# Where warming transposes, a masked copy, a run of products and a price in the planner stand: a two-layer hybrid encoder on one core

## The chip, the core and the metric

The kernel runs on one core of a Trainium2 chip. Five engines run side by side, each with its own queue in which instructions start in order: TensorE (PE: matrix products and transposes, with PEld for the loading of the stationary operand), VectorE (DVE), ScalarE (ACT), GpSimd (POOL) and SyncE (SP), which here issues the DMAs. TensorE writes to PSUM; VectorE and ScalarE read it there. Semaphores order the engines among each other. The metric is the device time of one execution in microseconds (us), lower is better.

## The reference

The trunk takes `x` of 512 frames by 1024 and puts 16 meta tokens in front of them (the zero pads of the reference need no work). It runs two layers, each a normed input projection, two groups of mixers, SiLU gates, an output projection and a residual, and ends with a norm.

```python
for layer in range(DEPTH):                     # DEPTH = 2
    hn = rms_norm(h, norm_g[layer])
    if layer % 2 == 0:
        out = layer_ab(hn, ...)                # top-k sparse attention (A) and gated linear attention (B)
    else:
        out = layer_cd(hn, ...)                # retention (C) and stick-breaking attention (D)
    h = h + jnp.where(valid[None, :, None], out, 0.0)
return rms_norm(h[:, PAD_FRONT + N_META:], final_g)
```

The change touches the chunked recurrences of B and C. B, cut to its core (C is alike, with a fixed decay and a layer norm of each head):

```python
def gla_chunked(q, k, v, log_a):               # 4 heads, chunks of 64, dk = 64, dv = 128
    bcum = jnp.cumsum(log_a, axis=3)
    q_t, k_t = q * jnp.exp(bcum), k * jnp.exp(-bcum)
    att = jnp.where(causal, jnp.einsum('bhncd,bhnsd->bhncs', q_t, k_t), 0.0)
    o_intra = jnp.einsum('bhncs,bhnse->bhnce', att, v)
    contrib = jnp.einsum('bhncd,bhnce->bhnde', k * jnp.exp(b_last - bcum), v)
    _, S_before = lax.scan(lambda S, inp: (S * inp[0][..., None] + inp[1], S), S0, (decay, contrib))
    o_inter = jnp.einsum('bhncd,bhnde->bhnce', q_t, S_before)
    return o_intra + o_inter
```

## The kernel before

**Layout.** All activations lie transposed: features on the 128 partitions, T = 528 tokens (16 meta, 4 blocks of 128 frames) along the free dimension, in two halves of 272 and 256. Each fp32 operand of a projection is split into a high and a low fp32r part, and a product is three: high by high, low by high, high by low (`begin` and `project`, from L603). The weights come as raw tiles by DMA; ScalarE makes the high part `wh`, VectorE the low part `wl` (`split_next`, L577).

**Recording and planning.** The program isn't issued as it is written. `Recorder.add` (L174) records each operation with what it reads and writes, and `price` (L216) gives it a cost in ns; for TensorE `o.mm` holds the rows, whether it is plain fp32, and the time after which the next one can start. A PSUM tile counts as one region in the dependencies, so whatever reads or writes any part of it stands in order with a write by another engine. `order` (L286) then plays all five engines forward in a list schedule: of the instructions that are ready on an engine it takes the one that can start first (on TensorE with a `MARGIN` of 300 ns, and 2000 ns of preference for the same rows, `STAY`), and among those the one that is due earliest. `LAT` is added between engines. An instruction on VectorE, ScalarE or GpSimd may start before the one ahead of it has ended, by `OVER` (84, 103 and 60 ns). A kind of tile has a fixed number of buffers, which go round in recorded order. What comes out is the order of the instructions on each engine; their waits are then made from the real dependencies. So a price changes no instruction, but it can change the order of all of them.

**Tiles of PSUM.** `acc` has 2 buffers of 1024 columns; `s()` and `tr()` share kind `x` with 3 buffers, and `pv()` is kind `y` with one buffer (L498).

**The start.** `consts` (L673) records 46 (`WARM`, L496) transposes of the identity into a y tile that nobody reads; they keep TensorE busy while the input comes. `load_x` (L728) then loads the meta tokens and `x` by rows, squares and norms them, turns the rows of the norm weights (`rows`, a tile from two DMAs of `norm_g` and `gla_gate_b`) with one transpose into `gains` (L789 to 791), and turns the 16 groups of `x` (`turn`), where ScalarE and VectorE apply the gains and make `hh` and `hl`.

**Layer one** runs the index scores, then top-k on VectorE (`topk`, rounds of MAX8 and MATCH_REPLACE8 on the tiles `score`, which the profile calls lt), while TensorE goes on with the values, the four heads of gated linear attention and their projections. Then come the eight heads of attention in pairs. In `gla_steps` (L1355) each head makes `att` (masked with `copy_predicated`), turns its keys, does the meta tokens in one tile `m` (a product, a masked copy into `attm`, a transpose of the meta keys into another part of `m`, a copy of it into `ktm`, then two products with the meta values `vm`), makes the states `ss` in seven dependent steps on VectorE (the profile calls them st, read from `x`), and sums the two parts of the output in a y tile:

```python
m = self.tr()
nc.tensor.matmul(m[:NMETA, 0:16], ks[:, :NMETA], qs[:, :NMETA], start=True, stop=True)
nc.vector.copy_predicated(attm[:NMETA], self.tri[:NMETA, :NMETA], m[:NMETA, 0:16])
self.transpose(m[:NMETA, 384:512], kh[:, :NMETA])
```

**Layer two** has retention heads (`retention_steps`, L1582) between pairs of stick-breaking heads, with the same two products per block: `av` by `vt` (the profile: y<-gv,wt) and `qx` by `ss` (y<-st,st). An fp32 product is two records in the profile.

As the recorder issues everything from one place, all instructions have line L406 in the profile; they are told apart by their tiles.

Of the kernel before, what the change touches and what calls it, by code (L numbers as in the profile page):

```python
# [16 lines left out]
P = 128  # L17
DM = 1024
KT = DM // P
NMETA = 16  # L20
SEQ = 512
T = NMETA + SEQ
NB = SEQ // P
# [15 lines left out]
def blk(b):  # L39
    return slice(NMETA + P * b, NMETA + P * (b + 1))  # L40
# [126 lines left out]
class Recorder:  # L167
# [48 lines left out]
    def price(self, o):  # L216
        o.mm, o.port = None, False
        n = max([x.free() for x in o.ins + o.outs] or [1])
        sbuf = not any(x.tile.psum for x in o.ins)
        scalar = 65 if any(isinstance(x, View) and x.free() == 1 for x in o.ins) and n > 1 else 0  # L220
        if o.eng == "tensor":
            lhs, rhs = (o.args[1], o.args[2]) if len(o.args) > 2 else (o.kw["lhsT"], o.kw["rhs"])
            turn = o.name == "transpose"
            plain = rhs.dtype == F32
            k, m, n = lhs.shape[0], lhs.free(), rhs.free()
            two = plain and not turn
            o.mm = (32 if k <= 32 else 64 if k <= 64 else P, plain, max(n * 0.45 * (2 if two else 1) + 4, 107 * m / P + 4) + (107 if two and n <= P else 0))
            o.cost = max(273, 170 + 0.4375 * n) if not two else 180 + 1.62 * n
        elif o.eng == "scalar":
            o.cost = (205 if sbuf else 165) + 0.83 * n + (80 if isinstance(o.kw.get("bias"), View) or isinstance(o.kw.get("scale"), View) else 0)  # L230
            if "accum_out" in o.kw:
                o.cost += 200
        elif o.eng == "vector":
            o.port = sbuf and o.name not in ("max", "match_replace")
            if o.name == "tensor_tensor_scan":
                o.cost = 144 + 2.1 * n
            elif o.name in ("tensor_scalar", "tensor_copy") and sbuf:
                o.cost = 160 + 0.52 * n + scalar
            elif o.name == "memset":
                o.cost = 100 + 0.3 * n  # L240
            else:
                o.cost = 148 + 1.05 * n + scalar
            if o.name == "tensor_tensor_reduce" or "accum_out" in o.kw:
                o.cost += 80
            if o.name == "match_replace":
                o.cost += 70
        elif o.eng == "gpsimd":
            o.cost = {"memset": 92 + 0.84 * n, "tensor_tensor": 178 + 2.17 * n}.get(o.name, 194 + 1.5 * n)
        else:
            x = o.outs[0] if o.outs else o.ins[0]  # L250
            kb = n * x.shape[0] / 256
            o.cost = kb * 3.6


    LAT = {"tensor": 55, "vector": 33, "scalar": 34, "gpsimd": 60, "sync": 27}
    OVER = {"vector": -84, "scalar": -103, "gpsimd": -60}
    SWITCH, ROWS = 80, 95
    MARGIN = 300
    STAY = 2000
# [26 lines left out]
    def order(self):  # L286
# [10 lines left out]
        wire = 0.0  # L297
        begun = {}
        result = []

        def ready(o):
            est = 0.0
# [13 lines left out]
        while left:  # L316
            best = None
            for e, xs in lists.items():
                pick = None
                base = free[e] + (last.mm[2] if e == "tensor" and last is not None else 0)  # L320
                for o in xs:
                    est = o.est
                    ok = True
                    for t in o.tiles:
                        if t.slot:
                            continue
                        k = t.kind
                        if t.at != k.next or not k.free:
                            ok = False
                            break  # L330
                        est = max(est, min(k.free)[0] + self.LAT[e])
                    if not ok:
                        continue
                    now = free[e] + (self.slot(last, o) if e == "tensor" and last is not None else 0)
                    start = max(est, now)
                    pri = o.pri
                    if e == "tensor" and last is not None:
                        pri -= self.STAY if o.mm[0] == last.mm[0] else 0
                    key = (max(est + (self.MARGIN if e == "tensor" else 0) - base, 0.0), pri)
                    if pick is None or key < pick[0]:  # L340
                        pick = (key, start, o)
                if pick and (best is None or pick[1] < best[1]):
                    best = pick
            assert best, "no instruction can be placed"
            _, start, o = best
            e = o.eng
            lists[e].remove(o)
            cost = o.cost
            if e == "vector" and o.port and begun.get("pool", (0, 0))[0] < start < begun.get("pool", (0, 0))[1] - 100:
                cost += begun["pool"][1] - start - 70  # L350
            if e == "gpsimd" and begun.get("port", (0, 0))[0] < start < begun.get("port", (0, 0))[1] - 100:
                cost += begun["port"][1] - start - 100
            end = start + cost
            if e == "vector" and o.port:
                begun["port"] = (start, end)
            ends[o] = end
            o.begin, o.end = start, end
            if e == "tensor":
                free[e], last = start, o
            elif e == "sync":  # L360
                free[e] = start + 430
                wire = end = max(wire, start + 1900) + o.cost
                if o.outs and o.outs[0].tile.whole and o.ins and o.ins[0].tile.whole:
                    end = start + 6900
                ends[o] = o.end = end
            else:
                free[e] = end + self.OVER[e]
                if e == "gpsimd":
                    begun["pool"] = (start, end)
            for t in o.tiles:  # L370
                k = t.kind
                if not t.slot:
                    t.slot = min(k.free)
                    k.free.remove(t.slot)
                    k.next += 1
            for t in o.tiles:
                t.left -= 1
                t.ends = max(t.ends, end)
                if not t.left:
                    t.kind.free.append((t.ends, t.slot[1]))  # L380
            result.append(o)
            left -= 1
            for q in o.succs:
                q.wait -= 1
                if not q.wait:
                    ready(q)
# [23 lines left out]
class Kernel:  # L410
# [82 lines left out]


    XL, XC, XN, XW, PW, PL = 2, 9, (0, 1, 1, 2), (1, 4, 7, 10, 13), 0, 0
    WARM = 46  # L496

    LAG = {"a": 5, "d": 6, "t": 1, "v": 4, "n": 9, "s": 6, "k": 11}  # L498
    TOPY = 3
# [173 lines left out]
    def consts(self):  # L673
        nc, ins = self.nc, self.ins
# [1 line left out]
        self.ident = self.cp.tile([P, P], F32, name="ident")  # L676
        make_identity(nc.core, self.ident.real)

        warm = self.pv()
        for _ in range(self.WARM):  # L680
            self.transpose(warm[:, :P], self.ident)
        self.one = self.cp.tile([P, 1], F32, name="one")
        nc.vector.memset(self.one, 1.0)
        self.eps = self.cp.tile([P, 1], F32, name="eps")
# [2 lines left out]
        self.gains = self.cp.tile([P, 18], F32, name="gains")  # L687
        self.g = self.gains[:, :16].rearrange("p (l k) -> p l k", l=2)
        self.gb = self.gains[:, 16:18]

    def late_consts(self):
        nc, ins = self.nc, self.ins
# [35 lines left out]
    def load_x(self):  # L728
        nc, ins = self.nc, self.ins
# [59 lines left out]
        t = self.tr()  # L789
        self.transpose(t[:, :18], rows)  # L790
        nc.scalar.copy(self.gains, t[:, :18])
        self.split_next()
        todo = [(g, t0, k, c) for g, t0, c in ((first, 0, self.HALVES[0]), (second, T0, self.HALVES[1]))
                for k in range(KT)]
# [560 lines left out]
    def gla_steps(self, head, r, v, gates, ep, qs, ks, kh):  # L1355
        nc = self.nc
# [17 lines left out]

        m = self.tr()
        nc.tensor.matmul(m[:NMETA, 0:16], ks[:, :NMETA], qs[:, :NMETA], start=True, stop=True)
        nc.vector.copy_predicated(attm[:NMETA], self.tri[:NMETA, :NMETA], m[:NMETA, 0:16])
        self.transpose(m[:NMETA, 384:512], kh[:, :NMETA])
        ktm = self.ktm[head % 2][:, :64]
        nc.vector.tensor_copy(ktm[:NMETA], m[:NMETA, 384:448])  # L1380
        yield self.LAG["t"]
# [21 lines left out]
        o = self.pv()  # L1403
        ov = o.rearrange("p (b e) -> p b e", b=NB)
        for b in range(NB):
            c = slice(P * b, P * (b + 1))
            nc.tensor.matmul(ov[:, b], att[:, b], vt[:, c], start=True, stop=False)
            nc.tensor.matmul(ov[:, b], qs[:, blk(b)], ss[:, c], start=False, stop=True)
        on = self.head_norm(ov, P, False)
        yield self.LAG["n"]  # L1410
        while not gates:
# [170 lines left out]
    def retention_steps(self, head, r, v, gates, q, k, qx, kz, kzm, turned):  # L1582
# [27 lines left out]
        o = self.pv()  # L1610
        ov = o.rearrange("p (b e) -> p b e", b=NB)
        for b in range(NB):
            c = slice(P * b, P * (b + 1))
            nc.tensor.matmul(ov[:, b], av[:, b], vt[:, c], start=True, stop=False)
            nc.tensor.matmul(ov[:, b], qx[:, c], ss[:, c], start=False, stop=True)
        on = self.head_norm(ov, P, True)
        yield self.LAG["n"]
        while not gates:
# [213 lines left out]
```

## Time and profile before

| what | us |
|---|---|
| median of 3 runs | 649.28 (648.82 to 650.77) |
| the profiled execution | 647.35 |
| its span, from first to last instruction | 645.6 |

The profile describes the execution of 647.35 us. Its last stretch and the largest wait by total:

```profile
580.00:645.60 65.60, 59.02 (x292) 48.55 (x290) 33.76 (x56) 28.51 (x63) 5.96 (x4) 0.97 0.33 113
```

```profile
POOL pm L406 <- ACT wt L406: 90.3, 18, 22.6
```

The first line is a stretch of the span in us: its length, then busy time and number of instructions of PE, PEld, DVE, ACT and POOL, the clock that TensorE was granted (1.00 is full), the share of the DMA engines and GB/s. The second says who waited for whom, with total, number and longest wait in us; idle time of an engine that isn't the bound, as POOL here, costs nothing. Matmuls are pipelined, and the end of one is modelled, so those that follow each other overlap in the records. A timeline row has the start, the duration, the engine, the operation, the tiles written and read, and in brackets how long the engine stood idle before it and what released it; "x3" means three such instructions in a row.

### The profile page before, as it was taken

What the parts mean: (1) busy time and instruction counts of PE and PEld (TensorE: products, weight loads), DVE (VectorE), ACT (ScalarE), POOL (GpSimd) and SP (SyncE); (2) the same over time, 40 slices, a digit from 0 to 9 for tenths busy, and PEclk for the clock granted to TensorE, in tenths of its full rate; (3) what the DMA queues carried; (4) which work ended last, traced back from release to release, by engine and by line L of the source; (5) the groups of instructions that cost most, each with busy time, mean ns of one, the idle gap of its engine ahead of it and who ended that gap; (6) DMA issues with size and microseconds to landing.
All of it is one profiled execution on the core that took longest, in us unless ns stands there. A gap on an engine that the chain in (4) does not pass through costs nothing. (4 is left out here: it accounts for less than half of the span.)

```text
span 645.6 us, 12173 instructions
## 1 busy us (share of the span) xinstructions
PE 620.5 (96%) x4393; PEld 569.2 (88%) x4393; DVE 491.6 (76%) x1142; ACT 412.9 (64%) x936; POOL 77.5 (12%) x185
## 2 busy tenths in 40 slices
PE   7999999899899999999899999989999999999995
PEld 6979999789889999999899999878888878988884
DVE  6768799999997786879732854789965689978443
ACT  5656562352344878799733775899854699956234
POOL 4001101100000111212121200000400010310030
PEclk9899999999999999999999999999999999999998
DMA  8437223222223323121243362103222203144503
GB/s 260 96 89 233 66 67 83 66 69 77 73 62 83 102 67 83 51 66 50 84 133 99 116 209 85 50 17 103 79 85 65 81 2 98 45 120 147 164 16 130
DMA packets 91103, 59.24 MB, mean 92 GB/s; under 512 B 7314, under 2 KB 81628, under 8 KB 91044
## 3 DMA queue, kind: packets, MB, share of 16 engines
q1 hardware_dynamic: 91044, 58.48, 31.6%
q8 instruction: 34, 0.56, 0.4%
q14 instruction: 25, 0.20, 0.1%
HBM read 53.18 MB, written 6.90 MB: 93 GB/s over the span
## 5 line engine op out<-in xcount | busy, mean ns | idle before, releaser
L406 PE MATMUL acc<-hh,wh 128*128 128x272 f32 (+2 forms) x968 | 243.7, 311 | 2.3 <-ACT hh L406 1.7
L406 PE MATMUL acc<-hl,wh 128*128 128x272 f32 (+2 forms) x968 | 236.1, 304 | 0.5 <-DVE hl L406 0.5
L406 PE MATMUL acc<-hh,wl 128*128 128x272 f32 (+2 forms) x968 | 232.6, 302 | 0.0
L406 PEld LDWEIGHTS acc<-hh,wh 128*128 128x128 f32 x968 | 159.1, 189 | 9.0 <-ACT hh L406 2.1
L406 PEld LDWEIGHTS acc<-hl,wh 128*128 128x128 f32 x968 | 158.1, 189 | 4.7 <-DVE hl L406 1.2
L406 PEld LDWEIGHTS acc<-hh,wl 128*128 128x128 f32 x968 | 157.1, 189 | 5.4
L406 ACT ACTIVATE wh<-raw 128x512 fp32r<-128x512 f32 x154 | 96.4, 630 | 101.8 <-PE acc L406 86.3
L406 DVE TENSOR_TENSOR wl<-raw,wh 128x512 fp32r<-128x512 f32 x154 | 106.1, 696 | 49.0 <-ACT wh L406 45.1
L406 ACT ACTIVATE wt<-x 128x272 f32<-128x272 f32 (+3 forms) x100 | 42.8, 451 | 29.5 <-PE x L406 15.9
L406 PE MATMUL x<-st,st 128*128 128x272 f32 (+6 forms) x240 | 51.3, 291 | 0.4 <-DVE ptm L406 0.2
L406 ACT ACTIVATE wt<-wt 128x528 f32<-128x528 f32 (+3 forms) x74 | 43.9, 603 | 8.7 <-DVE wt L406 7.7
L406 PE MATMUL x<-ident,wt 128*128 128x128 f32 (+1 forms) x296 | 45.3, 275 | 1.9 <-ACT wt L406 1.1
L406 PEld LDWEIGHTS x<-st,st 128*128 128x128 f32 (+2 forms) x240 | 37.4, 186 | 9.2 <-ACT wt L406 3.1
L406 PEld LDWEIGHTS x<-ident,wt 128*128 128x128 f32 (+1 forms) x296 | 33.8, 139 | 6.5 <-DVE ptm L406 1.9
L406 ACT ACTIVATE wt<-wt,tiny 128x272 f32<-128x272 f32 (+6 forms) x64 | 34.5, 561 | 7.8 <-POOL tiny L406 5.8
L406 ACT ACTIVATE st<-acc 64x528 fp32r<-64x528 f32 (+1 forms) x58 | 34.8, 599 | 1.3 <-DVE lt L406 0.4
L406 PE MATMUL y<-pt,vt 128*128 128x256 f32 x192 | 30.8, 283 | 1.9 <-ACT pt L406 1.8
L406 DVE TENSOR_TENSOR pt<-x,pt 128x384 fp32r<-128x384 f32 (+1 forms) x48 | 28.3, 595 | 4.7 <-ACT pt L406 4.3
L406 DVE TENSOR_TENSOR_SCAN wt<-wt,wt 128x64 f32<-128x64 f32 (+5 forms) x50 | 30.6, 657 | 0.1
L406 PEld LDWEIGHTS y<-pt,vt 128*128 128x128 f32 x192 | 26.0, 189 | 4.7 <-ACT pt L406 2.2
L406 POOL COPY pm<-wt 128x16 f32<-128x16 f32 x32 | 12.8, 419 | 140.1 <-ACT wt L406 90.3
L406 ACT ACTIVATE wt<-wt,one 128x528 f32<-128x528 f32 (+3 forms) x42 | 29.5, 703 | 0.2
(204 smaller groups left out, 922.1 us busy)
## 6 DMA issues: line engine op xcount, KB each, us to landing
raw<-in_w_in_ab_dram SPq DMA_DIRECT2D x64, 256.0 KB, 2.8
raw<-in_w_in_cd_dram SPq DMA_DIRECT2D x56, 256.0 KB, 2.9
raw<-in_w_out_ab_dram SPq DMA_DIRECT2D x16, 256.0 KB, 2.8
raw<-in_w_out_cd_dram SPq DMA_DIRECT2D x16, 256.0 KB, 2.7
rep<-rows SPq DMA_DIRECT2D x8, 328.0 KB, 5.9
lt<-rep SPq DMA_DIRECT2D x8, 264.0 KB, 2.7
pt<-in_x_dram SPq DMA_DIRECT2D x8, 256.0 KB, 4.4
wt<-in_x_dram SPq DMA_DIRECT2D x8, 256.0 KB, 3.1
```

The source lines that it names most:

```text
L406: getattr(getattr(self.core, o.eng), o.name)(*[bind(x) for x in o.args], **{k: bind(x) for k, x in o.kw.items()})
```

## The change

It has four parts.

1. `WARM` becomes two numbers, 26 and 20. A new function `warm(i)` records that many transposes of the identity into a y tile; `consts` calls it for the 26, and `load_x` for the 20, after the gains' transpose and its copy. In `price`, a transpose into a y tile takes 160 ns of TensorE instead of the 111 that the formula gives.
2. In `gla_steps`, the transpose of the meta keys is recorded before the masked copy of the same tile `m`.
3. In `gla_steps` and `retention_steps`, the four products with the values come first and the four with the states after them, instead of in turn. Only the first product of the bank has the start mark.
4. `order` remembers which PSUM tiles the last instruction on VectorE and on ScalarE read (`reads`). Where the next one reads the same tile, its start moves by 98 ns on VectorE and by 115 ns on ScalarE (`SAME`).

```diff
@@ -226,6 +226,8 @@
             two = plain and not turn
             o.mm = (32 if k <= 32 else 64 if k <= 64 else P, plain, max(n * 0.45 * (2 if two else 1) + 4, 107 * m / P + 4) + (107 if two and n <= P else 0))
             o.cost = max(273, 170 + 0.4375 * n) if not two else 180 + 1.62 * n
+            if turn and o.outs[0].tile.kind.tag == "y":
+                o.mm = (P, plain, 160)
         elif o.eng == "scalar":
             o.cost = (205 if sbuf else 165) + 0.83 * n + (80 if isinstance(o.kw.get("bias"), View) or isinstance(o.kw.get("scale"), View) else 0)
             if "accum_out" in o.kw:
@@ -254,6 +256,8 @@
 
     LAT = {"tensor": 55, "vector": 33, "scalar": 34, "gpsimd": 60, "sync": 27}
     OVER = {"vector": -84, "scalar": -103, "gpsimd": -60}
+
+    SAME = {"vector": 98, "scalar": 115}
     SWITCH, ROWS = 80, 95
     MARGIN = 300
     STAY = 2000
@@ -297,6 +301,7 @@
         wire = 0.0
         begun = {}
         result = []
+        reads = {}
 
         def ready(o):
             est = 0.0
@@ -332,6 +337,8 @@
                     if not ok:
                         continue
                     now = free[e] + (self.slot(last, o) if e == "tensor" and last is not None else 0)
+                    if e in self.SAME and reads.get(e, set()) & set(x.tile for x in o.ins if x.tile.psum):
+                        now += self.SAME[e]
                     start = max(est, now)
                     pri = o.pri
                     if e == "tensor" and last is not None:
@@ -354,6 +361,8 @@
             if e == "vector" and o.port:
                 begun["port"] = (start, end)
             ends[o] = end
+            if e in self.SAME:
+                reads[e] = {x.tile for x in o.ins if x.tile.psum}
             o.begin, o.end = start, end
             if e == "tensor":
                 free[e], last = start, o
@@ -493,7 +502,7 @@
 
 
     XL, XC, XN, XW, PW, PL = 2, 9, (0, 1, 1, 2), (1, 4, 7, 10, 13), 0, 0
-    WARM = 46
+    WARM = 26, 20
 
     LAG = {"a": 5, "d": 6, "t": 1, "v": 4, "n": 9, "s": 6, "k": 11}
     TOPY = 3
@@ -676,9 +685,7 @@
         self.ident = self.cp.tile([P, P], F32, name="ident")
         make_identity(nc.core, self.ident.real)
 
-        warm = self.pv()
-        for _ in range(self.WARM):
-            self.transpose(warm[:, :P], self.ident)
+        self.warm(0)
         self.one = self.cp.tile([P, 1], F32, name="one")
         nc.vector.memset(self.one, 1.0)
         self.eps = self.cp.tile([P, 1], F32, name="eps")
@@ -687,6 +694,11 @@
         self.gains = self.cp.tile([P, 18], F32, name="gains")
         self.g = self.gains[:, :16].rearrange("p (l k) -> p l k", l=2)
         self.gb = self.gains[:, 16:18]
+
+    def warm(self, i):
+        t = self.pv()
+        for _ in range(self.WARM[i]):
+            self.transpose(t[:, :P], self.ident)
 
     def late_consts(self):
         nc, ins = self.nc, self.ins
@@ -789,6 +801,7 @@
         t = self.tr()
         self.transpose(t[:, :18], rows)
         nc.scalar.copy(self.gains, t[:, :18])
+        self.warm(1)
         self.split_next()
         todo = [(g, t0, k, c) for g, t0, c in ((first, 0, self.HALVES[0]), (second, T0, self.HALVES[1]))
                 for k in range(KT)]
@@ -1374,8 +1387,8 @@
 
         m = self.tr()
         nc.tensor.matmul(m[:NMETA, 0:16], ks[:, :NMETA], qs[:, :NMETA], start=True, stop=True)
+        self.transpose(m[:NMETA, 384:512], kh[:, :NMETA])
         nc.vector.copy_predicated(attm[:NMETA], self.tri[:NMETA, :NMETA], m[:NMETA, 0:16])
-        self.transpose(m[:NMETA, 384:512], kh[:, :NMETA])
         ktm = self.ktm[head % 2][:, :64]
         nc.vector.tensor_copy(ktm[:NMETA], m[:NMETA, 384:448])
         yield self.LAG["t"]
@@ -1403,9 +1416,9 @@
         o = self.pv()
         ov = o.rearrange("p (b e) -> p b e", b=NB)
         for b in range(NB):
-            c = slice(P * b, P * (b + 1))
-            nc.tensor.matmul(ov[:, b], att[:, b], vt[:, c], start=True, stop=False)
-            nc.tensor.matmul(ov[:, b], qs[:, blk(b)], ss[:, c], start=False, stop=True)
+            nc.tensor.matmul(ov[:, b], att[:, b], vt[:, P * b:P * (b + 1)], start=b == 0, stop=False, skip_group_check=True)
+        for b in range(NB):
+            nc.tensor.matmul(ov[:, b], qs[:, blk(b)], ss[:, P * b:P * (b + 1)], start=False, stop=True, skip_group_check=True)
         on = self.head_norm(ov, P, False)
         yield self.LAG["n"]
         while not gates:
@@ -1610,9 +1623,10 @@
         o = self.pv()
         ov = o.rearrange("p (b e) -> p b e", b=NB)
         for b in range(NB):
+            nc.tensor.matmul(ov[:, b], av[:, b], vt[:, P * b:P * (b + 1)], start=b == 0, stop=False, skip_group_check=True)
+        for b in range(NB):
             c = slice(P * b, P * (b + 1))
-            nc.tensor.matmul(ov[:, b], av[:, b], vt[:, c], start=True, stop=False)
-            nc.tensor.matmul(ov[:, b], qx[:, c], ss[:, c], start=False, stop=True)
+            nc.tensor.matmul(ov[:, b], qx[:, c], ss[:, c], start=False, stop=True, skip_group_check=True)
         on = self.head_norm(ov, P, True)
         yield self.LAG["n"]
         while not gates:
```

## The prediction

> **What bounds the kernel now.** I read the page's head first, then busy time by stretches, then what TensorE waited for. Columns of the stretches: length, then busy time and count of PE, weight loads, DVE, ACT, POOL, then granted clock, DMA share, GB/s.
>
> ```profile
> span 645.6 us, 12173 instructions
> ```
>
> ```profile
> PE 620.5 (96%) x4393; PEld 569.2 (88%) x4393; DVE 491.6 (76%) x1142; ACT 412.9 (64%) x936; POOL 77.5 (12%) x185
> ```
>
> ```profile
> 80.00:196.00 116.00, 109.40 (x880) 104.30 (x879) 111.70 (x318) 49.14 (x109) 6.83 (x18) 1.00 0.27 69
> 196.00:310.00 114.00, 112.74 (x914) 110.32 (x912) 93.41 (x274) 93.02 (x223) 19.94 (x59) 1.00 0.27 73
> 320.00:420.00 100.00, 100.00 (x752) 95.64 (x752) 54.87 (x112) 59.59 (x139) 13.89 (x21) 1.00 0.37 112
> ```
>
> ```profile
> PE x L406 <- DVE attm L406: 3.7, 2, 2.2
> PE y L406 <- DVE st L406: 1.8, 2, 1.1
> ```
>
> TensorE is the bound: 645.6 - 620.5 = 25.1 us of idle is all that any reordering can win. From 320 to 420 it never stops. The stretch from 80 to 196, where top-k and linear attention share VectorE, is different: VectorE is busy for 111.70 of 116 us, and TensorE stands still for 6.6 us. Of these, 3.7 + 1.8 = 5.5 us are two named waits (total us, times, longest), both in the linear attention that the change edits.
>
> **Part 1, the warming.** These rows are the chain at the start, in order of time (start, duration).
>
> ```profile
> 3.53 0.43 SPq L406 DMA_DIRECT2D mid<-in_norm_g_dram  x1
> 9.25 0.23 PE L406 MATMUL x<-ident,mid 18*128 18x18 f32 x1
> 9.52 0.17 ACT L406 COPY gains<-x 128x18 f32<-128x18 f32 x1 [1.50 <-PE x L406]
> 10.86 1.27 DVE L406 TENSOR_SCALAR pt<-pt,tiny 128x512 f32<-128x512 f32 x3
> 11.40 0.55 PE L406 MATMUL x<-ident,pt 128*128 128x128 f32 x3 [0.95 <-DVE pt L406]
> 12.31 0.39 PE L406 MATMUL acc<-hh,wh 128*128 128x272 f32 x1 [0.36 <-ACT hh L406]
> 13.20 0.39 PE L406 MATMUL acc<-hl,wh 128*128 128x272 f32 x1 [0.50 <-DVE hl L406]
> ```
>
> ```profile
> DMA to landing us min/median/max: 4.2/4.2/4.2
> ```
>
> ```profile
> L406 PE MATMUL y<-ident x46: 272/399/475, 1.6 to 9.0; 128*128 128x128 f32 x46
> ```
>
> In two half-us windows, the warming transposes alone (length, busy time and count, clock, DMA share, GB/s):
>
> ```profile
> 5.50:6.00 0.50, 0.50 (x4) 1.00 0.93 352
> 8.00:8.50 0.50, 0.50 (x7) 1.00 0.92 306
> ```
>
> The gains' transpose runs at 9.25, behind all 46 warming transposes. ACT, in order, stood 1.50 us before the gains' copy, with a weight split and the last block's norm behind it; VectorE (10.86), TensorE (11.40) and the first product (12.31) follow. The norm weights had landed at 3.53 + 4.2 = 7.7, so the queue of warming set 9.25. The gate bias, issued half a us later, is then estimated at 8.2.
>
> How much earlier it goes depends on the planner, not on the recorded place. It starts warming at 0, so 26 at the new price of 160 ns reach 4.2 us. By its own formulas (430 ns per issue, 3.6 ns per KB) it expects the gains' rows at 6.5 us; it takes what is ready first, with 300 ns of margin, and the second warming batch is ready at once, for it depends on nothing but its tile. It sees the first batch end at 4.27, starts the second 0.06 later and could place a next instruction at 4.49: (6.51 + 0.30 - 4.49) / 0.16 rounds up to 15, so the first and 15 more of the 20 go ahead of the gains too; only 4 move behind. In the late warming a window of 0.5 us touches 7 transposes of 0.27 us in flight, so they start (0.5 + 0.27) / 7 = 0.11 us apart. So 4 x 0.11 = **0.4 us** at the start, between 0 (the bias rows or the first weight tile land late) and 1.0 (from 9.25 to 8.2, the landing, if all 20 go behind). The four that move cost nothing: they stand before a wait for VectorE of 0.95 us. The price of 160 itself moves nothing else, as no other transpose writes a y tile.
>
> The clock is the larger matter in this stage.
>
> ```profile
> 13.00:20.00 7.00, 6.80 (x29) 5.63 (x30) 5.33 (x16) 3.17 (x11) 0.00 (x0) 0.54 0.74 174
> 20.00:26.00 6.00, 6.00 (x46) 5.59 (x46) 4.48 (x11) 4.46 (x10) 0.00 (x0) 0.97 0.01 1
> ```
>
> A mean clock of 0.54 over 7 us and 0.97 over 6 is half clock for 2 x (0.46 x 7 + 0.03 x 6) = 6.8 us. Kept warm, at most 3.4 us would go; VectorE needs 5.33 of the first 7 us, so 7 - 5.33 = 1.7 us is the nearer value. I count none of it: with 4 transposes moved, the thin stretch, with its waits of 0.95, 0.36 and 0.50 us up to 13.20, shifts by 0.4 us and stays as thin.
>
> By the Trainium skill ("TensorE: Matmul & The Clock Gate", Part 4: PE-mode transpose) transposes do not count as busy for the clock, and warming could do nothing. The windows of the warming above, where the count goes from 4 to 7 per half-us under transposes alone, disagree. By the rule the clock's term is 0, by the rows 0 to 3.4 us.
>
> **Part 2, the meta transpose ahead of the masked copy.** Two heads in order of time:
>
> ```profile
> 116.67 0.15 DVE L406 COPY_PREDICATED attm<-tri,x 16x16 f32<-16x16 int32 x1
> 116.88 0.28 PE L406 MATMUL x<-ident,st 128*16 128x128 f32 x1 [1.56 <-DVE attm L406]
> 117.75 0.20 DVE L406 COPY ktm<-x 16x64 f32<-16x64 f32 x1
> 118.07 0.43 PE L406 MATMUL x<-vmz,ktm 128*64 128x128 f32 x2
> ```
>
> ```profile
> 126.88 0.34 DVE L406 SCALAR_TENSOR_TENSOR st<-st,lt,x 64x128 f32<-64x128 f32 x1
> 127.27 0.49 PE L406 MATMUL y<-st,st 128*128 128x128 f32 x2 [0.79 <-DVE st L406]
> ```
>
> ```profile
> 170.95 0.28 PE L406 MATMUL x<-ident,st 128*16 128x128 f32 x1 [2.16 <-DVE attm L406]
> 181.48 0.49 PE L406 MATMUL y<-st,st 128*128 128x128 f32 x2 [1.05 <-DVE st L406]
> ```
>
> The transpose writes the tile that the masked copy reads, so TensorE stood 1.56 and 2.16 us for a copy that VectorE reached late. This wait goes entirely. What is late next is the ktm product: 118.07 - 1.56 = 116.5, but VectorE can end the ktm copy at 116.67 + 0.15 + 0.20 = 117.0 at best. So about 1.0 of the first 1.56 us is won there, and the same of the second by analogy: 2.0. Further on stands the product on the last state (127.27), released by VectorE, which does not run sooner. In an unchanged order its wait would grow by what was won, and nothing would be left; VectorE is full, its work is the same. Bounds: 0, and 3.7.
>
> **Part 3, all att products before the state products.** Same count, same shapes, one start mark per bank. The product that waits at 127.27 and 181.48 is the last on the state, and it already has the other seven ahead of it. The reorder hides nothing of it directly: 0, at most the 1.8 us if the planner now finds other work to put between.
>
> **Part 4, the price of a repeated PSUM read.** Is it real?
>
> ```profile
> 12.65 1.31 DVE L406 SCALAR_TENSOR_TENSOR hl<-x,gains,hh 128x272 fp32r<-128x272 f32 x3
> 102.13 4.00 DVE L406 SCALAR_TENSOR_TENSOR st<-acc,wt 64x256 f32<-64x256 f32 x12
> 208.21 1.44 DVE L406 TENSOR_TENSOR kl<-acc,st 64x528 fp32r<-64x528 f32 x2 [1.80 <-ACT st L406]
> ```
>
> ```profile
> L406 DVE TENSOR_TENSOR kl<-acc,st 64x528 fp32r<-64x528 f32 x16 | 11.3, 705 | 13.9 <-ACT st L406 13.7
> L406 DVE SCALAR_TENSOR_TENSOR hl<-x,gains,hh 128x272 fp32r<-128x272 f32 x8 | 3.7, 498 | 2.4 <-ACT hh L406 2.4
> ```
>
> Three reads of different tiles take 1.31, less than 3 x 0.498 = 1.49: they overlap by 0.09 each. Two reads of one tile take 1.44, more than 2 x 0.705: no overlap. So it is. The planner has believed VectorE early by 12 x 0.098 = 1.2 us after the run at 102, about the 1.56 us by which it came late at 116. No instruction gets faster; but with the price, the planner should set free projection products before the late copies and state steps. It changes the whole order of all engines from the first such read on. For the 5.5 us of waits in linear attention I take 2.0 us won, parts 2 to 4 together (ends 0 and 5.5; the nearest row is the 1.0 per head above). For the rest:
>
> ```profile
> PE x L406 <- POOL pm L406: 2.5, 3, 1.0
> PE y L406 <- ACT pt L406: 1.8, 3, 0.9
> PE acc L406 <- ACT hh L406: 1.4, 1, 1.4
> PE x L406 <- ACT wt L406: 1.3, 3, 0.5
> PE x L406 <- DVE ptm L406: 0.9, 2, 0.6
> ```
>
> These 7.9 us after 196 sit behind ACT chains that read one tile several times; a new order may mend or worsen them. I take 0.5 us, with 2.5 either way.
>
> **Sum.** 0.4 + 2.0 + 0.5 = 2.9 us. The profiled execution took 647.35 us (span 645.6 and 1.75 around it), so 644.5 on its footing; the median of the runs is 649.28, 1.93 above it, so **646.4 us**, own range 644.5 to 648.5.
>
> **Rivals.** (a) The stall only moves: VectorE stays full from 80 to 196, and the products on ktm and on the state wait as long as the copy did. For it: VectorE's 111.70 of 116. Against: TensorE has projections to place there, and runs ahead into a stretch where VectorE has slack (93.41 of 114). Only the start's 0.4 remains: 648.9. (b) The clock holds: more warming falls behind the gains than I count, or the thin stretch is split otherwise. For it: the waits in it add up to 1.8 us only. 649.28 - 2.9 - 1.7 = 644.7, down to 643.0 with the whole 3.4. (c) Slower: the masked copy now waits for the transpose too, and top-k is queued behind it on the full engine.
>
> ```profile
> 188.03 0.21 PE L406 MATMUL x<-st,st 128*16 128x16 f32 x2
> 188.57 0.16 DVE L406 COPY_PREDICATED attm<-tri,x 16x16 f32<-16x16 int32 x1
> ```
>
> VectorE came 0.5 us after the product here. If the planner sets half a projection between product and transpose (24 products; 320 to 420 shows 752 in 100 us, so 3.2 us), VectorE loses 2.7 us in such a head: 649.28 - 0.4 + 2.7 = 651.6, and 654.3 with two. It decides from a gap above 0.5 us; both being ready at once, the planner more likely sets them side by side.
>
> By the Trainium skill (the same page, What's actually happening) the clock is judged in free-running windows of 3.4 us. The 6.8 us agree with two; that only an idle window ends full clock does not, as no gap here exceeds 0.95 us. If the windows run free, (b) can also come in some executions and not in others.
>
> **How the numbers follow.** Forecast 0.48, (a) 0.25, (b) 0.15, (c) 0.12. About 0.3%, 1.95 us, is what a measurement of this kernel can tell from no change, so faster means below 647.3. Faster: 0.36 of the forecast, 0.15, and 0.03 of (a), 0.54. Slower: (c) 0.12, and 0.04 from the edges of forecast and (a), 0.16. Same: 0.30. The range 643.0 to 651.0 takes in (a), (b) and the new order's 2.5 us; it leaves out most of (c).
>
> **What would show it.** The gains' transpose near 8.8; 4 warming transposes behind it; half clock still there. No wait of TensorE on attm, a shorter one on st or a new one on ktm; TensorE's idle from 80 to 196 near 4.5 us. Wrong if that idle stays at 6.6, if idle after 196 grows by over 2 us, or if VectorE waits for the meta transpose.

## The result: 9.8 us less, and the profile after

| | before | after |
|---|---|---|
| median of 4 runs, us | 649.05 (648.71 to 650.77) | 639.22 (638.73 to 639.69) |
| the profiled execution | 647.35 | 638.82 |
| its span | 645.6 | 636.9 |

The ratio is 0.9843, with a 95% interval of 0.9823 to 0.9863. The forecast was 646.4, the range 643.0 to 651.0: the sign was right, and the time lies below the range. Both profiled executions were granted the same mean clock of TensorE, 0.992.

The head of the page after, with busy time and instructions by engine, and two stretches (length, busy time and count of PE, PEld, DVE, ACT, POOL, clock, DMA share, GB/s):

```profile
span 636.9 us, 12154 instructions
...
PE 617.1 (97%) x4393; PEld 569.9 (89%) x4393; DVE 491.5 (77%) x1142; ACT 412.1 (65%) x936; POOL 79.0 (12%) x185
```

```profile
80.00:196.00 116.00, 111.87 (x901) 106.74 (x900) 111.94 (x318) 49.68 (x110) 6.90 (x18) 1.00 0.28 72
196.00:310.00 114.00, 112.75 (x925) 111.24 (x924) 96.58 (x283) 96.10 (x232) 20.02 (x60) 1.00 0.27 75
```

What TensorE waited for after the change (total us, times, longest), the largest lines of 80 to 196 and of the rest:

```profile
PE y L415 <- DVE st L415: 3.1, 5, 1.2
...
PE x L415 <- DVE wt L415: 0.4, 1, 0.4
```

```profile
PE x L415 <- POOL pm L415: 2.6, 3, 1.2
PE acc L415 <- ACT hh L415: 1.4, 1, 1.4
PE acc L415 <- DVE wl L415: 0.7, 2, 0.4
```

Nothing waits on attm any more, the wait on st has grown from 1.8 to 3.1 us, and the idle time of TensorE between 80 and 196 went from 6.6 to 116 - 111.87 = 4.1 us. In the whole span it went from 25.1 to 19.8. That is 5.3 of 8.7 us; the other 3.4 stand as less busy time (620.5 to 617.1) for as many instructions. The end of a matmul is modelled, so a wait shorter than its time in flight (0.27 us and more, against a start every 0.12) is counted as busy. That the 3.4 us were such waits is likely but not shown: the profile doesn't set them apart from what it costs TensorE to go from one kind of product to another, and that order changed too.

Where the time went is read from instructions that both kernels have. The rows of two tiles, before and then after (ns at least, median, most; start of the first and of the last, us):

```profile
L406 DVE TENSOR_TENSOR lm<-x,lt x8: 156/157/163, 211.0 to 289.9; 16x16 f32<-16x16 f32 x8
L406 DVE TENSOR_TENSOR mx<-x,gt x16: 152/422/692, 136.7 to 603.8; 128x512 f32<-128x512 f32 x8, 128x16 f32<-128x16 f32 x8
```

```profile
L415 DVE TENSOR_TENSOR lm<-x,lt x8: 155/156/163, 208.0 to 284.7; 16x16 f32<-16x16 f32 x8
L415 DVE TENSOR_TENSOR mx<-x,gt x16: 152/423/692, 134.7 to 595.1; 128x512 f32<-128x512 f32 x8, 128x16 f32<-128x16 f32 x8
```

The first attention scores (lm, first start) come 3.0 us earlier, the last retention head (mx, last start) 8.7 us earlier, as much as the end. So 3.0 us were won up to the attention, and 5.7 after it, in stages that the edits of the recorded order hardly touch. The halves of the span, before and after, say in what form:

```profile
0.00:196.00 196.00, 185.87 (x1373) 173.72 (x1374) 169.22 (x439) 97.03 (x217) 18.32 (x63) 0.98 0.38 102
196.00:645.60 449.60, 434.63 (x3023) 395.48 (x3021) 322.42 (x703) 315.92 (x720) 59.21 (x122) 1.00 0.30 87
```

```profile
0.00:196.00 196.00, 188.80 (x1398) 176.25 (x1399) 169.93 (x441) 97.91 (x219) 18.32 (x63) 0.98 0.38 104
196.00:636.90 440.90, 428.29 (x2998) 393.67 (x2996) 321.53 (x702) 314.18 (x718) 60.69 (x122) 1.00 0.30 88
```

TensorE's idle time up to 196 us fell by 2.9 us (10.1 to 7.2), all that was won there; after 196 it fell by 2.4 (15.0 to 12.6), so of the 5.7 us the other 3.4 are the busy time.

### The profile page after: what moved, and what is told of

Its sections match the earlier page's. It is cut to its first block, busy times and chain, and to the rows that moved or that the text cites. A ratio compares the mean times of both kernels' runs of the same rounds, so it can differ in the third digit from the quotient of the medians.

```text
span 636.9 us, 12154 instructions
## 1 busy us (share of the span) xinstructions
PE 617.1 (97%) x4393; PEld 569.9 (89%) x4393; DVE 491.5 (77%) x1142; ACT 412.1 (65%) x936; POOL 79.0 (12%) x185
## 4 chain that ended last, share of the span: by engine, by line
PE 69%; ACT 14%; DVE 12%; issue 2%; SPq 1%; DMA 1%; POOL 0%; DVEq 0%; POOLq 0%; ACTq 0%
PE acc L415 50%; PE x L415 15%; ACT wt L415 7%; PE y L415 5%; DVE lt L415 3%; DVE wl L415 2%; DVE m L415 2%; ACT wh L415 2%; DVE st L415 1%; ACT st L415 1%; ACT pt L415 1%; DVE wt L415 1%; ACT low L415 1%; SPq L415 1%; DVE mx L415 1%
## 5 line engine op out<-in xcount | busy, mean ns | idle before, releaser
L415 PE MATMUL y<-pt,vt 128*128 128x256 f32 x192 | 27.7, 278 | 0.0
L415 DVE MATCH_REPLACE8 lt<-m,lt 128x400 f32<-128x400 f32 (+2 forms) x48 | 26.7, 559 | 0.2
```

The costliest lines, as they stand in the source:

```text
L415: getattr(getattr(self.core, o.eng), o.name)(*[bind(x) for x in o.args], **{k: bind(x) for k, x in o.kw.items()})
```

## The experiments

All are edits of the kernel before, but for no_price and full_spread, which are edits of the changed kernel; each was timed beside the kernel before on the same chip. The rival theories were these. **A**: the price tells the planner the truth about repeated reads, and the order becomes better where these stand. **B**: the moved transpose and products take the waits away. **C**: the order before was an unlucky one, and any other may be better. **D**: the planner only needed more slack on VectorE and ScalarE, wherever it is charged.

| run | median, us | before | ratio (95% interval) |
|---|---|---|---|
| only_warm | 649.73 | 650.04 | 0.9992 (0.9976 to 1.0009) |
| only_meta | 649.23 | 650.04 | 0.9981 (0.9966 to 0.9996) |
| only_products | 646.85 | 650.04 | 0.9953 (0.9934 to 0.9973) |
| only_price | 639.51 | 650.04 | 0.9826 (0.9805 to 0.9846) |
| no_price | 648.62 | 650.07 | 0.9979 (0.9964 to 0.9994) |
| price_vector | 641.41 | 649.19 | 0.9882 (0.9852 to 0.9912) |
| price_scalar | 643.24 | 649.19 | 0.9907 (0.9882 to 0.9933) |
| price_near | 639.64 | 649.19 | 0.9853 (0.9827 to 0.9879) |
| price_double | 639.89 | 651.18 | 0.9836 (0.9805 to 0.9866) |
| price_wrong | 643.60 | 649.19 | 0.9908 (0.9883 to 0.9932) |
| price_wrong5 | 642.67 | 650.07 | 0.9880 (0.9856 to 0.9904) |
| price_spread | 642.46 | 650.07 | 0.9886 (0.9867 to 0.9905) |
| spread_double | 643.23 | 650.28 | 0.9891 (0.9868 to 0.9914) |
| spread_less | 651.86 | 650.28 | 1.0033 (1.0017 to 1.0048) |
| price_shuffle | 645.61 | 650.07 | 0.9934 (0.9917 to 0.9951) |
| price_shuffle_b | 649.90 | 650.28 | 0.9989 (0.9973 to 1.0004) |
| price_shuffle_c | 649.88 | 650.28 | 0.9999 (0.9983 to 1.0015) |
| full_spread | 637.81 | 651.18 | 0.9807 (0.9783 to 0.9830) |

### Which part it is

Each of the four parts alone, as in the diff of the change, and the first three together (no_price).

```diff
 # only_price: part 4 and nothing else
+    SAME = {"vector": 98, "scalar": 115}
...
+                    if e in self.SAME and reads.get(e, set()) & set(x.tile for x in o.ins if x.tile.psum):
+                        now += self.SAME[e]
```

> Part 1 alone (26 and 20 warming transposes, the price of 160). Theory A (the truer price of a repeated PSUM read makes the order better) and theory B (the moved transpose and products take TensorE's waits away) both expect the start's 0.5 us and nothing else: 648.5. Theory C (any new order moves the time by some us, up or down, by chance) expects 645 to 652.

> Part 2 alone, the meta transpose ahead of the masked copy. A: the wait on attm goes, a later wait for VectorE takes its place, 648 to 649. B: 3.7 us of the waits on attm are won, 645.3. C: 643 to 652.

> Part 3 alone, att products before state products. A: nothing, 648.5 to 649.5, as the product that waits is the last one either way. B: at least the 1.8 us of waits on st, 647.2. C: 643 to 652.

> Part 4 alone, the price of a repeated PSUM read in the planner. A: most of the gain, 642 to 644, with the waits after 196 us (stick-breaking, attention) gone as in the changed kernel. B: little, 647 to 649. C: 643 to 655, not the same places.

> The change without part 4 (parts 1, 2 and 3 together). Theory A (the price makes the order): 646 to 648.5, what parts 1 to 3 gave alone (0, 0.8 and 3.2 us off). Theory C (chance of the order): 640 to 655.

The price alone gives 10.5 us, the whole gain and more than A expected; parts 1 to 3 together give 1.4 us. B falls. The meta transpose alone is worth only 0.8 us, and its timeline on TensorE shows why:

```profile
114.50 0.28 PE L406 MATMUL x<-ident,st 128*16 128x128 f32 x1
118.16 0.43 PE L406 MATMUL x<-vmz,ktm 128*64 128x128 f32 x2 [1.69 <-DVE attm L406]
...
171.68 0.43 PE L406 MATMUL x<-vmz,ktm 128*64 128x128 f32 x2 [2.19 <-DVE attm L406]
```

The transpose no longer waits, and the next product on the same copies waits instead: 1.69 and 2.19 us in place of 1.56 and 2.16. The products alone gave 3.2 us, where theory A expected nothing. That is the number that B expected, but not for its reason: the wait on st is 1.9 us, as before (1.8). Most of it is the clock, which the record gives for every execution with its span. Of the executions of the products alone, four of seven were granted 0.991 or 0.992 (spans 644.7 to 645.1); of the 22 of the kernel before beside them none was granted over 0.990 (646.4 to 647.7 at 0.990). At one clock the difference is smaller: 645.6 to 644.9 us in the profiled executions (both 0.992), and at 0.987 from 648.2, 648.3 and 648.7 to 646.8 and 647.1. With parts 1 and 2 beside it most of it is gone.

With the price alone, two heads on TensorE and VectorE:

```profile
115.03 0.21 PE L412 MATMUL x<-st,st 128*16 128x16 f32 x2
116.19 0.15 DVE L412 COPY_PREDICATED attm<-tri,x 16x16 f32<-16x16 int32 x1
116.40 0.28 PE L412 MATMUL x<-ident,st 128*16 128x128 f32 x1
```

```profile
167.13 0.21 PE L412 MATMUL x<-st,st 128*16 128x16 f32 x2
167.68 0.15 DVE L412 COPY_PREDICATED attm<-tri,x 16x16 f32<-16x16 int32 x1
167.99 0.27 PE L412 MATMUL x<-ident,st 128*16 128x128 f32 x1
```

The transpose still stands behind the copy here, yet TensorE doesn't stand still: neither row has an idle time, since other work was put between. The copy comes 1.2 us after the product that it reads (116.19 - 115.03) and 0.6 in the second head; before, the same product of the first head stood at 114.29:

```profile
114.29 0.21 PE L406 MATMUL x<-st,st 128*16 128x16 f32 x2
```

The copy came at 116.67, 2.4 us later. VectorE is no faster; the planner, which now takes it for slower, keeps the two engines closer together.

### Where it sits, by engine

```diff
-    SAME = {"vector": 98, "scalar": 115}
+    SAME = {"vector": 98}        # price_vector
+    SAME = {"scalar": 115}       # price_scalar
```

> Part 4 with the price on VectorE only (98 ns; none on ScalarE). Theory A (the gain comes from a truer price where a tile is read again): about half of the 10.5 us of the whole price, 643 to 646, with the gain sitting in linear attention from 80 to 196 us. Theory C (any other order may land there by chance): 638 to 655.

> Part 4 with the price on ScalarE only (115 ns; none on VectorE). A: the other half, 643 to 646, with the gain in the attention and the stick-breaking pairs after 196 us, nothing in linear attention. C: 638 to 655.

The first attention scores (first start) in price_vector and in price_scalar:

```profile
L412 DVE TENSOR_TENSOR lm<-x,lt x8: 151/156/158, 208.7 to 285.5; 16x16 f32<-16x16 f32 x8
```

```profile
L412 DVE TENSOR_TENSOR lm<-x,lt x8: 154/157/157, 210.8 to 288.0; 16x16 f32<-16x16 f32 x8
```

Against 211.0, VectorE's price wins 2.3 us up to there and ScalarE's 0.2: what is won in linear attention is VectorE's. But A expected VectorE's gain to sit there, and most of its 7.8 us comes later. The two alone are worth 7.8 and 5.9 us, and together 10.5, so they don't add up; each already does a part of what the other does. And up to the attention the place of the price makes no difference that shows. The same row in price_near (right places) and price_wrong5 (wrong places, see below), both with the clock of the kernel before in the first 26 us (0.87):

```profile
L412 DVE TENSOR_TENSOR lm<-x,lt x8: 151/158/159, 209.0 to 285.8; 16x16 f32<-16x16 f32 x8
```

```profile
L412 DVE TENSOR_TENSOR lm<-x,lt x8: 154/157/163, 209.0 to 286.0; 16x16 f32<-16x16 f32 x8
```

### Truth, slack or chance

```diff
 # price_near, price_double: the size at the right places
+    SAME = {"vector": 90, "scalar": 125}
+    SAME = {"vector": 196, "scalar": 230}
 # price_wrong, price_wrong5: the same prices at wrong places
-                    if e in self.SAME and reads.get(e, set()) & set(x.tile for x in o.ins if x.tile.psum):
+                    if e in self.SAME and o.at % 11 == 0:      # == 5 in price_wrong5
 # price_spread, spread_double, spread_less: no place at all
-    OVER = {"vector": -84, "scalar": -103, "gpsimd": -60}
+    OVER = {"vector": -75.4, "scalar": -92.5, "gpsimd": -60}   # -66.8, -82; -92.6, -113.5
 # price_shuffle, _b, _c: as many charged as let off
+                    if e in self.SAME:
+                        now += self.SAME[e] * {0: 1, 5: -1}.get(o.at % 11, 0)   # {3: 1, 8: -1}; {7: 1, 2: -1}
```

> Part 4 with 90 and 125 ns in place of 98 and 115. Most of the order on every engine comes out different, the price is still about right. A and D: as good, 638.5 to 642. C: it can land anywhere from 638 to 655, and a time above 644 would speak for chance.

> The same two prices at wrong places: on every eleventh recorded operation of VectorE and ScalarE, whatever it reads. As many are charged in all (some 95 and 81; the repeated reads number 92 and 81). A: no gain, 648 to 652. Theory D (the planner only needed more slack on these engines, wherever): as good as part 4, 640 to 643. C: 638 to 655.

> As the wrong places of before, with another eleventh of the operations. D: again 642 to 645. C: it scatters, 640 to 655; a difference of over 3 us from the first wrong places speaks for chance.

> The sum of part 4's price spread evenly: every operation of VectorE starts 8.6 ns later in the planner and every one of ScalarE 10.5 ns (98 x 92 / 1047 and 115 x 81 / 890). Theory D (slack on these engines, wherever): 640 to 644. Theory A: 647 to 651. C: 640 to 655.

> Twice the even price (17.2 and 21 ns per operation). D: at least as good as the even price once, 639 to 643. A: no better than once, 642 to 646, as the planner is now slower than the chip in the places that read no tile twice.

> The even price with the other sign: every operation of VectorE starts 8.6 ns sooner in the planner, every one of ScalarE 10.5 ns. D: worse, 650 to 656. C: 643 to 650, like any other order.

> No slack in the mean: every eleventh operation of VectorE and ScalarE is charged 98 or 115 ns, and another eleventh is let off as much. The order of all engines changes. A and D: 647 to 652. C (the order before was an unlucky one, and most others are better): 641 to 646.

> A second order without slack in the mean: another eleventh charged, another let off. Theory C (the order before was an unlucky one, and most others are better by 3 to 5 us): 643 to 647. Theory A with D (only slack or a true price helps): 647 to 652.

> A third such order, with the same expectations: C 643 to 647, A with D 647 to 652. With the first two and with no price, it shows how far orders scatter for no reason.

> Part 4 alone with twice the price (196 and 230 ns) at the repeated reads. A (the right size at the right place): worse than once, 640 to 646, as these reads are now overpriced. D (more slack is better until it is enough): 638 to 642.

Three things follow. First, **slack**: the same sum charged at either of two sets of wrong places is worth 0.92 and 1.20%, spread evenly it is worth 1.14%, and the even price with the other sign costs 0.33%, with an interval that excludes no change. Twice the even price is worth no more than once (1.09%). So D is right for about two thirds of the gain; that A expected nothing of wrong places was a miss. Second, **place**: at the repeated reads the price is worth 1.74%, and its interval doesn't meet that of the even price; another 8 to 10 ns (1.47%) and twice the size (1.64%) also win more than either of the wrong places and either of the even prices, though the first one's interval (0.9827 to 0.9879) overlaps theirs. That speaks for A in the last third. Third, **chance**: three orders without slack in the mean gave 0.66, 0.11 and 0.01%, and the first of them, 645.61, landed where C expected it. Orders scatter by up to 4.5 us (650.07 - 645.61) for no reason that was found, and that bounds what any one of these runs says alone; the last third (2.9 to 4.9 us) is of that size, so A's part isn't shown. C as the main cause falls, since the nine runs with part 4 alone or another price of that sign all lie lower than any of these three.

A part of the differences is the clock. In the 22 executions of the kernel before that were timed beside the first four runs, the ten granted 0.990 span 646.4 to 647.7 us, and the eight granted 0.982 span 649.2 to 650.0: some 0.3 us for each 0.001. The price at its places was granted 0.991 to 0.993, at the first wrong places 0.986 to 0.988. A line through all executions on record, with one level for each kernel, has 0.32 us for each 0.001. Put on one clock by it, which is an estimate, the price wins 8.8 us (price_near 8.8, price_double 9.3), the wrong places 6.7 and 6.6, the even price 6.4 and 7.1, and the three orders without slack 3.1, 1.1 and -0.4. Slack is then about three quarters of the gain, and place some 2 us.

### Do the two add up

The whole change and the even price on top of it.

> The whole change and the even price on top (8.6 and 10.5 ns per operation). If what the even price wins is the same as what the repeated reads' price wins, no better than the change: 638.5 to 642. If the two add up, 633 to 637, and it beats both kernels.

637.81, a ratio of 0.9807. It is the fastest run, but its interval overlaps the change's own: the two gains are mostly one, and that it beats the change isn't shown.

## Why the prediction was right and wrong

- **The start, 0.4 us: right.** The rows after, on TensorE and then ScalarE's copy:

```profile
8.72 0.23 PE L415 MATMUL x<-ident,mid 18*128 18x18 f32 x1
8.80 0.27 PE L415 MATMUL x<-ident,gv 16*128 16x16 f32 x2
9.01 0.65 PE L415 MATMUL y<-ident 128*128 128x128 f32 x4
```

```profile
11.78 0.39 PE L415 MATMUL acc<-hh,wh 128*128 128x272 f32 x1 [0.36 <-ACT hh L415]
```

  The gains go at 8.72 instead of 9.25 (8.8 was expected), four warming transposes come behind them, and the first product starts 0.5 us earlier. By itself this part can't be told from no change.
- **The half clock: right that it stays.** The same two stretches after:

```profile
13.00:20.00 7.00, 7.00 (x32) 5.85 (x32) 5.08 (x15) 3.16 (x10) 0.00 (x0) 0.53 0.77 181
20.00:26.00 6.00, 6.00 (x47) 5.50 (x47) 4.75 (x10) 5.01 (x12) 0.00 (x0) 1.00 0.03 5
```

  0.53 over 7 us is 2 x 0.47 x 7 = 6.6 us at half clock, against 6.8. Rival (b) did not happen in this execution. The length is not the same in all: the first 26 us of no_price, with the same two batches of warming, and of only_price, with the warming of before (0.87 there):

```profile
0.00:26.00 26.00, 22.92 (x139) 20.04 (x140) 17.80 (x47) 16.52 (x44) 6.56 (x31) 0.93 0.63 174
```

```profile
0.00:26.00 26.00, 21.99 (x127) 19.71 (x127) 16.07 (x43) 14.72 (x40) 6.58 (x31) 0.80 0.64 173
```

  That is 2 x 0.07 x 26 = 3.6 us of half clock in the one and 10.4 in the other; nothing here ties it to the warming.
- **Parts 2 and 3, nothing by themselves in an unchanged order: right for part 2,** which alone moved its wait, as rival (a) had it (0.8 us in the median). For part 3 alone, 3.2 us in the median were not foreseen; most of them are the clock of the executions, and 0.7 to 1.5 us are left at one clock. Rival (c) did not happen: VectorE's waits between 80 and 196 us after the change are one of 1.2 us for ScalarE and one of 0.3 for TensorE at a state, none for the transpose.
- **Parts 2 to 4 in linear attention, 2.0 us of the 5.5: right,** 2.5 (3.0 less the start's 0.5). The reason given holds as far as VectorE ran behind the plan and other products now stand before the late copies. That it takes the price at the repeated reads isn't shown, since wrong places win as much up to there (209.0 in both rows above). The wait on st grew to 3.1 us, where a shorter one or one on ktm was expected.
- **Part 4 after 196 us, "0.5 us, with 2.5 either way": wrong.** This term was mis-sized; it measured 5.7 us in the profile. The step that failed is the one that took TensorE's recorded waits for all that an order can win ("25.1 us of idle is all that any reordering can win", and the 7.9 us in five lines after 196). The idle time after 196 fell by 2.4 us, which the 2.5 would have held; the other 3.4 came out of busy time, which the sum put at nothing. Behind that, the price was taken for a correction of some reads at their places (92 on VectorE and 81 on ScalarE by the count of the experiments), whose effect elsewhere would go either way. The runs show that charging the same sum on both engines at any place wins 5.6 to 7.6 us in the medians (6.4 to 6.7 at one clock). That the planner was too hopeful on both engines throughout is the likely reading; its times and the trace weren't compared instruction by instruction.
- The profiled execution won 8.5 us, the medians 9.8. The rest is in the medians before: they lie 1.7 us above its profiled execution, the median after 0.4. The clock can account for it: the four executions after were granted 0.992 and 0.993, while of the 22 of the kernel before beside the first four experiments none got over 0.990, against 0.992 in the profiled one. For the four of the table of the result the record doesn't list it.

## What to carry to other kernels

In a list schedule with in-order queues, a planner that believes an engine too fast can make the engine behind it wait, also in places that a profile doesn't name; so a sum of the named waits is no upper bound on what a better order wins, and the planner's pace is worth comparing with the trace before single instructions are moved. Moving one instruction off a wait on a full engine moved the wait here to the next one on the same engine. And measure a new price beside the same price in wrong places and beside orders without any, and compare at one clock: here that told slack from chance, and truth from slack only in part.

## What was unexpected in the hardware

The clock halves after waits of 1 to 2 us in the middle of the kernel, in some executions and not in others. only_warm has the order of the kernel before on VectorE and ScalarE, and on TensorE but for the warming; its clock in five stretches, and that of before in the first two:

```profile
116.00:118.00 2.00, 0.83 (x5) 0.83 (x6) 2.00 (x8) 0.98 (x2) 0.49 (x1) 0.83 0.00 0
118.00:120.00 2.00, 2.00 (x10) 1.32 (x9) 2.00 (x7) 0.00 (x0) 0.05 (x1) 0.50 0.36 70
120.00:122.00 2.00, 2.00 (x15) 1.70 (x14) 1.56 (x5) 0.27 (x1) 0.00 (x0) 0.81 0.21 61
...
322.00:324.00 2.00, 2.00 (x12) 2.00 (x11) 2.00 (x4) 1.97 (x5) 0.00 (x0) 0.53 0.03 8
324.00:326.00 2.00, 2.00 (x13) 2.00 (x12) 0.53 (x1) 0.68 (x3) 1.24 (x1) 0.61 0.02 6
```

```profile
116.00:118.00 2.00, 1.12 (x9) 1.04 (x9) 2.00 (x8) 0.69 (x2) 0.54 (x1) 1.00 0.00 0
118.00:120.00 2.00, 2.00 (x16) 1.55 (x15) 2.00 (x5) 0.00 (x0) 0.00 (x0) 1.00 0.48 120
```

The first takes 2 x (0.17 + 0.50 + 0.19) = 1.7 us of full clock, just behind the wait on attm (1.57 us); the second, behind the wait for hh at the end of attention (1.35 us), as much. The kernel before has both waits too, 1.56 and 1.35 us, and keeps the full clock there. What each cost is read from rows of VectorE that stand in the same order in both, before and then only_warm (the first two of before, at 117.75 and 126.88, are in the prediction):

```profile
318.99 0.71 DVE L406 TENSOR_TENSOR hl<-mx,hh 128x528 fp32r<-128x528 f32 x1 [0.71 <-ACT hh L406]
327.66 0.71 DVE L406 TENSOR_TENSOR lt<-acc,wt 128x528 f32<-128x528 f32 x1 [1.81 <-PE acc L406]
```

```profile
118.03 0.20 DVE L408 COPY ktm<-x 16x64 f32<-16x64 f32 x1
128.21 0.34 DVE L408 SCALAR_TENSOR_TENSOR st<-st,lt,x 64x128 f32<-64x128 f32 x1
320.44 0.71 DVE L408 TENSOR_TENSOR hl<-mx,hh 128x528 fp32r<-128x528 f32 x1 [0.71 <-ACT hh L408]
330.64 0.71 DVE L408 TENSOR_TENSOR lt<-acc,wt 128x528 f32<-128x528 f32 x1 [1.80 <-PE acc L408]
```

only_warm is 0.3 us late at the first row and 1.3 at the second, 1.5 at the third and 3.0 at the fourth: the two half clocks cost 1.0 and 1.5 us. So a wait of 1.4 us can cost 2.9. The change took away the waits on attm but not the one for hh (1.4 us in its table of waits), and in full_spread, which has that wait as well, the clock is 0.50 from 314 to 316 us; that the change has rid the kernel of this scatter (0.96 us between the fastest and the slowest run after, 2.06 before) isn't shown by four runs. The 3.4 us at half clock each agree with one window of the Trainium skill ("TensorE: Matmul & The Clock Gate", What's actually happening); that the window has to be idle does not, with TensorE idle for 1.2 us of the two at 116 and busy around it.
